# The MLP of a hybrid transformer block rewritten as one ordered sequence of 224 block products

## The chip, the core and the metric

One core of a Trainium2 chip runs the whole block. TensorE (PE in the profile) multiplies into PSUM; VectorE (DVE), ScalarE (ACT) and GpSimd (POOL) work on tiles of 128 partitions; SyncE (SP) issues nearly all DMA transfers, some are issued by ScalarE. The metric is device time in microseconds for one execution, median of three runs.

## The reference

One layer: norm, a mixer (attention and a linear recurrence) with output projection, norm, and an MLP with squared ReLU. Sequence and model width are 1024, the MLP is 4096 wide, all in float32.

```python
def rms_norm(x, g):
    xf = x.astype(jnp.float32)
    y = xf * lax.rsqrt(jnp.mean(xf * xf, axis=-1, keepdims=True) + EPS)
    return (y * g.astype(jnp.float32)).astype(x.dtype)
...
def sq_relu_mlp(h, w_up, w_down):
    return jnp.square(jax.nn.relu(h @ w_up)) @ w_down
...
        h = rms_norm(x, norm1_g[l])
        x = x + hybrid_mixer(h, w_in[l], conv_w[l], conv_b[l], w_rg[l], b_rg[l], w_ig[l], b_ig[l],
                             lru_lambda[l], q_norm_g[l], k_norm_g[l], w_out[l])
        h = rms_norm(x, norm2_g[l])
        x = x + sq_relu_mlp(h, w_up[l], w_down[l])
```

## The kernel before, in words

Every float32 product is made of three matmuls. Each operand is split into a high part (a cast to fp32r by ScalarE) and a low part (operand minus high part, by VectorE or GpSimd); low x high, high x low and high x high are summed in PSUM (`mm3`, lines 62 to 65; `mmc`, lines 602 to 605).

Up to some 450 us the kernel runs the input projection, the recurrence and the attention; its results go to a DRAM buffer `mix_d`. Then comes the output projection (lines 532 to 575): for two column halves `n` and eight token tiles `t`, weights `wr_o` and mixed rows `mr` are loaded through a ring of four tiles of 1024 columns (pool `raws`), split, multiplied into a bank `po`, and added to `x`, which stays in SBUF as `x1`. In the second half, after every second token tile, `x1` is transposed and scaled into `h2` (the MLP's input, model width on partitions), and the row norms go to `rs2`.

The MLP works on blocks. Both `h2 @ w_up` and the product with `w_down` are 2 x 2 block products done with seven block multiplications instead of eight (Strassen-Winograd), for two groups `g` of 2048 MLP columns. So sums and differences of blocks of weights and of `h2` have to be built before they are split, and results are combined in `U` (8 x 4 tiles of 512 columns) or, on the way down, in PSUM and `x1`. Here `hb(k, t, u)` is a piece of `h2`: model half `k`, token half `t`.

Up group (lines 626 to 715), three passes of eight steps `j`: `t2`, `t1`, `t3` with summed weights; `b11`, `b22`, `b21` with plain or reloaded weights (`s2_d` in DRAM); `t4`. Evictions are spread over ScalarE and VectorE; the squared ReLU is `relu2` (line 633). Down group (lines 719 to 804), four passes of eight steps `k`: `da`, `db`, `dd`, `df`. Here the banks `pa` (four) collect several products, `pb` or `pc` (four) one; `acc` (line 732) adds a finished bank to `x1`.

Raw loads, high and low parts are pairs of 512 columns in one tile of 1024 (`raw`, `pair`, `split`); low parts go to VectorE, and every third of some to GpSimd (`lo_eng`, line 597). The rings: four raw tiles, six moving pairs, three stationary pairs.

The order on each engine is set by the framework: it takes the program's instructions, simulates a timeline, and puts each engine's instructions in the order of that timeline. Engines then run in order and wait on semaphores. Tiles that are laid over memory of released pools wait until the former users are done.

## Time and profile before

| what | value |
|---|---|
| median of three runs | 1246.22 us (1245.65 to 1248.36) |
| profiled execution: own time | 1246.13 us |
| profiled execution: span | 1244.3 us |
| PE busy | 1145.4 us (92%), 5410 matmuls |
| DVE busy | 898.2 us (72%) |
| ACT busy | 574.6 us (46%) |
| POOL busy | 657.8 us (53%) |
| granted TensorE clock, mean | 0.966 |
| first MLP matmul, last MLP matmul's eviction | 578.69 us, 1237.83 us |

The span is counted from the first to the last instruction; the execution's own time is a little more. "Busy" counts a matmul from its start to its modelled end, and matmuls overlap, so a busy share near 100% is not a pitch. A row of a timeline has start, duration, engine, line, operation, output and inputs, and in brackets how long the engine sat idle before it and what ended the wait. A row of a window has the stretch, its length, busy time and instruction count for each engine, the granted clock, the DMA share and GB/s.

### The profile page before, as it was taken

How to read it: one execution, taken by the hardware profiler on the slowest of the kernel's cores; microseconds unless marked ns; L12 is line 12 of the kernel's file. 1: busy time of each engine (PE TensorE's matmuls, PEld its weight loads, DVE VectorE, ACT ScalarE, POOL GpSimd, SP SyncE). 2: the span in 40 equal slices, each digit the busy share in tenths (PEclk: the TensorE clock that was granted, in tenths of full speed). 3: DMA queues.
4: the chain of work that ended last, by engine and by line, in shares of the span. 5: the costliest groups of instructions: out<-in, count | busy, mean ns of one | idle time of the engine just before them, and what ended most of it. 6: DMA issues, size and time to landing. Idle time of an engine off the chain costs nothing.

```text
span 1244.3 us, 15625 instructions
## 1 busy us (share of the span) xinstructions
PE 1145.4 (92%) x5410; PEld 940.1 (76%) x5410; DVE 898.2 (72%) x1248; ACT 574.6 (46%) x1023; POOL 657.8 (53%) x552
## 2 busy tenths in 40 slices
PE   8998899899999969973999997999989899989998
PEld 7876687789887658863877876878868688768786
DVE  6889998999988865236466676876954756968744
ACT  7555466566655641243354543243333544523331
POOL 1366654644465743015346679744533475996450
PEclk9999999999999879996998998999999899989999
DMA  8210011401010833002433252455134223425633
GB/s 257 56 39 35 35 47 33 133 10 49 10 33 27 276 111 133 1 1 101 127 94 93 68 169 93 159 177 161 53 127 129 83 79 125 135 94 170 196 134 119
DMA packets 80144, 123.55 MB, mean 99 GB/s; under 512 B 9616, under 2 KB 28096, under 8 KB 80064
## 3 DMA queue, kind: packets, MB, share of 16 engines
q1 hardware_dynamic: 75456, 114.15, 29.3%
q10 hardware_dynamic: 4608, 8.39, 1.7%
q8 instruction: 43, 0.70, 0.2%
q14 instruction: 37, 0.30, 0.1%
HBM read 103.64 MB, written 18.88 MB: 98 GB/s over the span
## 4 chain that ended last, share of the span: by engine, by line
PE 46%; DVE 19%; POOL 11%; DMA 9%; issue 8%; ACT 5%; SPq 1%; POOLq 0%; ACTq 0%; DVEq 0%
PE p L605 16%; PE pa L605 6%; PE po L63 2%; DVE g L415 2%; PE po L65 2%; PE po L64 2%; PE pc L605 2%; POOL U L637 2%; PE pd L63 2%; PE pd L64 2%; PE pd L65 2%; DMA de<-in_w_down_dram 1%; PE pb L605 1%; PE av L435 1%; DMA dc<-in_w_down_dram 1%
## 5 line engine op out<-in xcount | busy, mean ns | idle before, releaser
L416 POOL TENSOR_TENSOR w<-w,g 128x128 f32<-128x128 f32 (+3 forms) x96 | 100.0, 1051 | 102.8 <-DVE g L415 52.5
L415 DVE TENSOR_TENSOR_SCAN g<-g 128x128 f32<-128x128 f32 (+3 forms) x96 | 112.0, 1179 | 6.2 <-ACT g L410 4.6
L63 PE MATMUL pd<-wh_p,hTl 128*128 128x384 f32 x256 | 91.1, 357 | 9.5 <-DVE vv L180 5.0
L64 PE MATMUL pd<-wl_p,hTh 128*128 128x384 f32 x256 | 89.9, 351 | 0.3
L65 PE MATMUL pd<-wh_p,hTh 128*128 128x384 f32 x256 | 87.9, 343 | 0.0
L637 POOL TENSOR_TENSOR U<-U 128x512 f32<-128x512 f32 x48 | 67.9, 1417 | 36.5 <-ACT U L635 34.4
L605 PE MATMUL p<-mh_t,sl_s 128*128 128x512 f32 x128 | 50.4, 401 | 28.2 <-DVE sl_s L60 24.6
L605 PE MATMUL p<-mh_b,sl_a 128*128 128x512 f32 x128 | 52.1, 407 | 9.5 <-DVE U L690 9.5
L660 POOL TENSOR_TENSOR rq<-rs,rq 128x512 f32<-128x512 f32 x16 | 22.3, 1397 | 72.5 <-DMA rq<-in_w_up_dram 72.5
L430 ACT CAST wth<-pw 128x512 fp32r<-128x512 f32 (+1 forms) x80 | 42.6, 548 | 38.5 <-PE pw L426 26.8
L410 ACT ACTIVATE g<-z 128x128 f32<-128x128 f32 (+3 forms) x96 | 48.1, 501 | 25.9 <-PE z L408 11.0
L63 PEld LDWEIGHTS pd<-wh_p,hTl 128*128 128x128 f32 x256 | 49.2, 192 | 13.6 <-DVE vv L180 6.7
L60 DVE TENSOR_TENSOR wtl<-pw,wth 128x512 fp32r<-128x512 f32 (+1 forms) x80 | 49.5, 629 | 12.0 <-ACT wth L430 11.5
L426 PE MATMUL pw<-ident,w 128*128 128x128 f32 x288 | 48.7, 288 | 3.9 <-POOL w L416 1.8
L605 PE MATMUL p<-ml_b,sh_a 128*128 128x512 f32 x128 | 51.6, 403 | 0.0
L605 PE MATMUL p<-mh_b,sh_a 128*128 128x512 f32 x128 | 51.5, 402 | 0.0
L64 PEld LDWEIGHTS pd<-wl_p,hTh 128*128 128x128 f32 x256 | 49.3, 193 | 2.7 <-issue 1.4
L605 PE MATMUL p<-ml_t,sh_s 128*128 128x512 f32 x128 | 50.8, 397 | 0.0
L605 PE MATMUL p<-mh_t,sh_s 128*128 128x512 f32 x128 | 50.8, 397 | 0.0
L605 PEld LDWEIGHTS p<-mh_t,sl_s 128*128 128x128 f32 x128 | 24.8, 194 | 34.0 <-DVE sl_s L60 24.9
L60 DVE TENSOR_TENSOR sl_a<-ra,sh_a 128x1024 fp32r<-128x1024 f32 x16 | 24.8, 1550 | 35.1 <-ACT sh_a L516 35.1
L65 PEld LDWEIGHTS pd<-wh_p,hTh 128*128 128x128 f32 x256 | 49.1, 192 | 1.2 <-issue 1.2
(367 smaller groups left out, 3909.6 us busy)
## 6 DMA issues: line engine op xcount, KB each, us to landing
rs<-in_w_up_dram SPq DMA_DIRECT2D x32, 256.0 KB, 2.7
ra<-in_w_up_dram SPq DMA_DIRECT2D x16, 512.0 KB, 3.7
da<-in_w_down_dram SPq DMA_DIRECT2D x32, 256.0 KB, 3.5
db<-in_w_down_dram SPq DMA_DIRECT2D x32, 256.0 KB, 2.7
dd<-in_w_down_dram SPq DMA_DIRECT2D x32, 256.0 KB, 2.6
wr_p<-in_w_in_dram SPq DMA_DIRECT2D x24, 192.0 KB, 2.7
xt<-in_x_dram SPq DMA_DIRECT2D x8, 512.0 KB, 6.5
wr_o<-in_w_out_dram SPq DMA_DIRECT2D x8, 512.0 KB
```

The costliest lines, as they stand in the source:

```text
L60: eng.tensor_tensor(lo, src, hi.bitcast(F32), op=ALU.subtract)
L63: nc.tensor.matmul(ps, al, bh, start=start, stop=False)
L64: nc.tensor.matmul(ps, ah, bl, start=False, stop=False)
L65: nc.tensor.matmul(ps, ah, bh, start=False, stop=stop)
L410: nc.scalar.activation(g[:, :kn], z, AF.Sigmoid, scale=-1.0)
L415: nc.vector.tensor_tensor_scan(gr, gr, gr, g[:, kn:kn + 1], op0=ALU.mult, op1=ALU.bypass)
L416: nc.gpsimd.tensor_tensor(w[:, :kn], w[:, :kn], g[:, 1:kn + 1], op=ALU.mult)
L426: nc.tensor.transpose(pw[:, i * P:(i + 1) * P], wrow[rr][j // 4][:, j % 4 * P:(j % 4 + 1) * P], ident)
L430: nc.scalar.copy(wth[:, :nw], pw[:, :nw])
L605: nc.tensor.matmul(ps, x_, y_, start=start and n == 0, stop=stop and n == 2, skip_group_check=True)
L637: nc.gpsimd.tensor_tensor(c, c, c, op=ALU.mult)
L660: nc.gpsimd.tensor_tensor(q[:, 1], r[:, 1], q[:, 1], **add)
```

## The change

The MLP becomes one list of 224 block products of 12 matmuls each (`Product`; 112 per group), fed by `Item`s that load 1 to 4 raw tiles. All raw tiles, stationary parts and moving parts are now 512 columns wide and live in rings of 8, 6 and 12. After each product's matmuls the program writes its eviction, attached work, the sum for the product eight ahead, the stationary split six ahead (which also issues the loads for which tiles are free) and, on the way down, the moving split four ahead. From the fifth product on every instruction of PE, DVE, ACT, POOL and SP is kept in that written order (`keep_in_program_order`); the first four are still placed by the framework.

All high parts are ScalarE's, all low parts VectorE's. The passes are regrouped. Up: `b11`/`b21` (16 products, plain weights), `t2`/`b22`/`t3` (24, one item of four loads per `j`), `t1`/`t4` (16). The spill of `s2_d` is gone. Down: `da`/`db` (16), `ea`/`eb` (16), `ga`/`gc` (16), `ha` (8).

Before that, `mlp_head` is called in the output projection ahead of token tile 4 of the second half: it loads and splits the first operands there. For this the memory around the output projection is laid out anew: its raw ring has three tiles (was four), each weight piece has a pair of its own, and the rings lie on the right side of memory, over the last attention tiles. The removed bodies of `up_group` and `down_group` are printed above and are not repeated here.

```diff
-    rwp = pool(ctx, "raws", bufs=4)
-    mvp = pool(ctx, "moving", bufs=6)
-    stp = pool(ctx, "stationary", bufs=3)
+    raws = pool(ctx, "ra", bufs=4, side="right")
+    early = ExitStack()
+    wf = pool(early, "wf", bufs=4, side="right")
+    rwp = pool(early, "raws", bufs=3, side="right")
     tail = ExitStack()
+    wn0 = pool(tail, "wn0")
+    wn1 = pool(tail, "wn1")
+    junk = pool(tail, "junk").tile([P, D], F32, name="junk")
+    wn2 = pool(tail, "wn2", bufs=2)
     mxp = pool(tail, "mix")
     mixes = [(mxp.tile([P, KC, 512], F32R, name=f"mix{g}h"), mxp.tile([P, KC, 512], F32R, name=f"mix{g}l")) for g in range(2)]
+    wpools = {(0, u): wf for u in range(4)} | {(1, 0): wn0, (1, 2): wn1, (1, 3): wn2, (1, 1): wn2}
...
+    def wpair(n, u):
+        t = wpools[n, u].tile([P, 2, 2, 512], F32R, tag="w", name=f"wo{n}{u}")
+        return t[:, 0], t[:, 1]
...
+    MAHEAD, UAHEAD, WLAG, PINNED = 4, 8, 2, 4
+    pinned = False
...
+    rwr, stp, mvp = Ring(4, 4), Ring(3, 3), Ring(8, 4)
+    rwr.pools[0] = raws
+    class Engine:
+        def __init__(self, eng):
+            self.eng = eng
+        def __getattr__(self, op):
+            def call(*args, **kw):
+                ins = getattr(self.eng, op)(*args, **kw)
+                return tc.keep_in_program_order(ins) if pinned else ins
...
+    def split2(pl, name, src):
+        h, l = half(pl, name)
+        act.copy(h, src)
+        dve.tensor_tensor(l, src, h.bitcast(F32), **sub)
+        return h, l
...
+    QA, QB = (ps_z, ps_z, ps_d, ps_d), (ps_w, ps_w, ps_a, ps_t)
...
+    def mmc(ps, st, mv, start, stop):
+        for n, (x_, y_) in enumerate(((1, 0), (0, 1), (0, 0))):
+            pe.matmul(ps, st[x_], mv[y_], start=start and n == 0, stop=stop and n == 2, skip_group_check=True)
...
+        def load(self, q):
+            self.raws = [rwr.tile([P, 512], F32, tag="r", name=f"r_{name}") for name, _ in self.srcs]
+            for t, (_, src) in zip(self.raws, self.srcs):
+                sp.dma_start(t, src)
+            self.at = q
...
+            def mm():
+                b = ps()
+                for kc in range(4):
+                    c = slice(kc * P, kc * P + P)
+                    mmc(b, (pr.st[0][:, c], pr.st[1][:, c]), movs[f"{g}{key}"][kc], start and kc == 0, stop and kc == 3)
...
+        def pa_(j):
+            prod(its[j], 0, "b11", bks[j], lambda: act.copy(U[:, j, 1], bks[j]()), True, False, 1)
+        def pb_(j):
+            prod(its[j], 1, "b21", bks[j], lambda: relu2(j, 0, bks[j]()), False, True, 1)
+        pa_(0)
+        for j in range(1, 8):
+            pa_(j)
+            pb_(j - 1)
+        pb_(7)
...
+            after(q0 + 7 + u, lambda u=u: mov(f"{g}t2", u, U[:, u, 3]))
+            after(q0 + 9 + u, lambda u=u: dve.scalar_tensor_tensor(U[:, 4 + u, 2], U[:, u, 3], -1.0, hb(0, 0, u), op0=ALU.mult, op1=ALU.subtract))
+            after(q0 + 13, lambda u=u: mov(f"{g}b22", u, hb(1, 1, u)))
+            after(q0 + 15, lambda u=u: mov(f"{g}t3", u, U[:, 4 + u, 2]))
+        for j in range(8):
+            def sums(r):
+                tt(gps, r[1], r[1], r[0], **add)
+                tt(gps, r[2], r[2], r[1], **add)
+                tt(dve, r[3], r[3], r[2], **add)
+            it = Item([(f"sa{g}{j}", w(1, 0, j)), (f"sb{g}{j}", w(0, 0, j)), (f"sc{g}{j}", w(1, 1, j)), (f"sd{g}{j}", w(0, 1, j))], sums)
+            ITEMS.append(it)
+            ps, ps1 = banked(f"p2_{g}{j}"), banked(f"p3_{g}{j}")
+            prod(it, 2, "t2", ps, lambda j=j, ps=ps: tt(dve, U[:, j, 2], ps(), U[:, j, 1], **add), True, False, 1)
+            prod(it, 3, "b22", ps1, lambda j=j, ps1=ps1: tt(dve, U[:, j, 2], ps1(), U[:, j, 2], **add), True, True, 1)
+            prod(it, 1, "t3", ps, lambda j=j, ps=ps: tt(dve, U[:, j, 1], ps(), U[:, j, 1], **add), False, True, 2)
...
+            after(q0 + 21, lambda u=u: mov(f"{g}t1", u, hb(0, 1, u)))
+            after(q0 + 22, lambda u=u: mov(f"{g}t4", u, U[:, 4 + u, 3]))
+        for j in range(8):
+            it = Item([(f"ta{g}{j}", w(1, 0, j)), (f"tb{g}{j}", w(1, 1, j))], lambda r: tt(gps, r[0], r[0], r[1], **add))
+            ITEMS.append(it)
+            ps, ps1 = banked(f"p4_{g}{j}"), banked(f"p5_{g}{j}")
+            def ev(j=j, ps=ps):
+                tt(dve, U[:, j, 3], ps(), U[:, j, 1], **sub)
+                tt(dve, U[:, j, 2], U[:, j, 2], ps(), **sub)
+                relu2(j, 3)
+                relu2(j, 2, eng=gps)
+            def ev1(j=j, ps1=ps1):
+                tt(dve, U[:, j, 1], ps1(), U[:, j, 1], **sub)
+                relu2(j, 1)
+            prod(it, 0, "t1", ps, ev, True, True, 1)
+            prod(it, 1, "t4", ps1, ev1, True, True, 1)
...
+            it = Item([(f"da{g}{k}", wd(0, k, 0)), (f"db{g}{k}", wd(0, k, 1))], lambda r: tt(gps, r[1], r[1], r[0], **add))
+            ITEMS.append(it)
+            prod("pa", 0, k, "da", True, False, it, 0, 1, lambda: acc(sets["pa"], 0, 0, rs2))
+            prod("pb", 2, k, "db", True, False, it, 1, 1, lambda: acc(sets["pb"], 1, 1, rs2),
+                 lambda k=k: tt(gps, U[:, k, 2], U[:, k, 2], U[:, k, 3], **sub))
+        for k in range(8):
+            def sums(r):
+                tt(gps, r[0], r[0], r[1], **add)
+                tt(gps, r[0], r[0], r[2], **add)
+            it = Item([(f"ea{g}{k}", wd(0, k, 1)), (f"eb{g}{k}", wd(0, k, 0)), (f"ec{g}{k}", wd(1, k, 1))], sums)
+            ITEMS.append(it)
+            prod("pa", 2, k, "ea", False, False, it, 0, 2, lambda: acc(sets["pa"], 0, 1, nrs2),
+                 lambda k=k: tt(dve, U[:, k, 2], U[:, k, 2], U[:, k, 0], **sub), r2_d[g][k])
+            prod("pb", 0, k, "eb", False, True, it, 2, 1, lambda: acc(sets["pb"], 0, 1, rs2, True),
+                 lambda k=k: tt(gps, U[:, k, 0], U[:, k, 1], U[:, k, 2], **add))
+        for k in range(8):
+            it = Item([(f"ga{g}{k}", wd(1, k, 1)), (f"gb{g}{k}", wd(0, k, 1)), (f"gc{g}{k}", wd(1, k, 0))],
+                      lambda r: tt(gps, r[0], r[0], r[1], **add))
+            ITEMS.append(it)
+            prod("pa", 2, k, "ga", False, False, it, 0, 2, lambda: acc(sets["pa"], 1, 1, nrs2, True),
+                 lambda k=k: dve.scalar_tensor_tensor(U[:, k, 2], U[:, k, 2], -1.0, U[:, k, 3], op0=ALU.mult, op1=ALU.subtract))
+            prod("pc", 1, k, "gc", True, True, it, 2, 1, lambda: acc(sets["pc"], 0, 0, rs2, True))
...
+            it = Item([(f"ha{g}{k}", wd(1, k, 0)), (f"hb{g}{k}", r2_d[g][k])], lambda r: tt(gps, r[0], r[0], r[1], **add))
+            ITEMS.append(it)
+            prod("pa", 3, k, "ha", False, True, it, 0, 2, lambda: acc(sets["pa"], 1, 0, rs2, True))
...
+    def load_items(q):
+        nonlocal free, nload
+        while nload < min(limit, len(ITEMS)) and free >= len(ITEMS[nload].srcs):
+            ITEMS[nload].load(q)
+            free -= len(ITEMS[nload].srcs)
+            nload += 1
+    def stat(n):
+        nonlocal free
+        if n < len(PR):
+            pr = PR[n]
+            pr.item.add()
+            pr.stat()
+            if pr.mov is None:
+                free += pr.free
+        load_items(n - NSTAT)
+    def moving(n, q):
+        nonlocal free
+        if n < len(PR) and PR[n].mov is not None:
+            PR[n].item.add()
+            PR[n].mov()
+            free += PR[n].free
+        load_items(q)
+    def mlp_head():
+        early.close()
+        mvp.pools[0] = pool(ctx, "ma", bufs=8, side="right")
+        stp.pools[0] = pool(ctx, "sa", bufs=3, side="right")
+        load_items(-NSTAT)
+        for u in range(4):
+            mov("0b11", u, hb(0, 0, u))
+        for n in range(3):
+            stat(n)
+        for u in range(4):
+            mov("0b21", u, hb(1, 0, u))
...
+            if n == 1 and grp[0] == 4:
+                mlp_head()
...
-                    wo[u] = split((nc.gpsimd, nc.vector)[(u + n) % 2], pair(stp if n == 0 and u != 1 else mvp, f"o{n}{u}"), wr)
+                    wo[u] = split((nc.gpsimd, nc.vector)[(u + n) % 2], wpair(n, u), wr)
...
+    for pl, nm, n in ((rwr, "rb", 4), (stp, "sb", 3), (mvp, "mb", 4)):
+        pl.pools[1] = pool(ctx, nm, bufs=n)
...
+    limit = len(ITEMS)
+    load_items(-NSTAT)
+    for n in range(3, NSTAT):
+        stat(n)
+    for q, pr in enumerate(PR):
+        pinned = q >= PINNED
+        pr.mm()
+        pr.ev()
+        for fn in pr.after:
+            fn()
+        if q + UAHEAD < len(PR) and PR[q + UAHEAD].usum is not None:
+            PR[q + UAHEAD].usum()
+        stat(q + NSTAT)
+        moving(q + MAHEAD, q)
+        for it in ITEMS[:nload]:
+            if it.at <= q - WLAG:
+                it.add()
```

How this moves instructions, at three places. First, PE between the output projection (`po17` is its last bank, `pth` the transposes of `x1`) and the MLP. Before (`p6_00` is the first MLP bank):

```order
L65 MATMUL po17_6058<-mh_o11_5740,mix1h_5427 128x512
L566 MATMUL pth5_3_6004<-ident_79,x1_5411 128x128 x4
L566 MATMUL pth7_0_6085<-ident_79,x1_5411 128x128 x4
L566 MATMUL pth7_1_6092<-ident_79,x1_5411 128x128 x4
L566 MATMUL pth7_2_6099<-ident_79,x1_5411 128x128 x4
L566 MATMUL pth7_3_6106<-ident_79,x1_5411 128x128 x4
L605 MATMUL p6_00_6189<-mh_t200_6152,sl_s00_6185 128x512
```

After:

```order
L65 MATMUL po17_6109<-wo11_5749,mix1h_5440 128x512
L577 MATMUL p1_00_6230<-m0b110_5949,sb110_5961 128x512 x3
L577 MATMUL p1_00_6230<-m0b111_5952,sb110_5961 128x512 x3
L577 MATMUL p1_00_6230<-m0b112_5955,sb110_5961 128x512 x2
L905 MATMUL pth5_3_6057<-ident_79,x1_5411 128x128 x4
L905 MATMUL pth7_0_6136<-ident_79,x1_5411 128x128 x4
```

The first product (`m0b11`: parts of the first token half, `sb110`: parts of a plain weight block) now stands directly behind the projection, with the last transposes among the products.

Second, SP around the end of the attention, whose last outputs are the stores from `ob313` and `ob303`. Before, the first loads of the projection stand well ahead of them:

```order
L541 DMA wr_o00_5432<-in_w_out_dram 128x2x512
L546 DMA mr00_5438<-mix_d_87 128x2x512
L443 DMA mix_d_87<-ob213_4675 64x256
L467 DMA mix_d_87<-hl30_5329 128x512
L541 DMA wr_o02_5460<-in_w_out_dram 128x2x512
L546 DMA mr02_5466<-mix_d_87 128x2x512
```

After, they come behind both stores and behind four loads of the MLP:

```order
L443 DMA mix_d_87<-ob313_5103 64x256
L577 DMA r_a00_5941<-in_w_up_dram 128x512
L577 DMA r_b00_5942<-in_w_up_dram 128x512
L443 DMA mix_d_87<-ob303_5202 64x256
L577 DMA r_a01_5945<-in_w_up_dram 128x512
L577 DMA r_b01_5946<-in_w_up_dram 128x512
L880 DMA wr_o00_5448<-in_w_out_dram 128x2x512
L885 DMA mr00_5453<-mix_d_87 128x2x512
```

Third, the `t1`/`t4` pass after the change, VectorE (`p4`, `p5`: banks of the two products of a step; `st10`, `st41`: low parts for products six ahead):

```order
L577 TENSOR_TENSOR U_6199<-p4_01_7150,U_6199 128x512
L577 TENSOR_TENSOR U_6199<-U_6199,p4_01_7150 128x512
L577 TENSOR_TENSOR st10_7169<-r_ta04_6999,st10_7169 128x512
L577 TENSOR_TENSOR U_6199<-p5_01_7172,U_6199 128x512
L577 TENSOR_TENSOR st41_7188<-r_tb04_7000,st41_7188 128x512
```

and ScalarE in the same step (the rows of `U` are relu, square, relu, then relu, square):

```order
L577 ACTIVATE U_6199<-U_6199 128x512 x3
L577 CAST st10_7169<-r_ta04_6999 128x512
L577 ACTIVATE U_6199<-U_6199 128x512 x2
L577 CAST st41_7188<-r_tb04_7000 128x512
L577 ACTIVATE U_6199<-U_6199 128x512 x3
```

Each low part follows its cast, and each relu its subtract, in the same place of both rows. Before, VectorE's subtracts of the last up pass (`L714`) stood in ones and twos between splits of 1024 columns, as the framework's timeline had placed them.

316 lines of the change are left out of this document (123 added, 193 removed).

## The prediction

> **What bounds the kernel now.** I read the windows first, cut at the stages, with TensorE beside the others.
>
> ```profile
> core 0: us, PE busy (x) PEld busy (x) DVE busy (x) ACT busy (x) POOL busy (x), PEclk, DMA share, GB/s
> 500.00:552.00 52.00, 51.09 (x252) 42.20 (x251) 12.04 (x46) 18.70 (x41) 0.00 (x0) 1.00 0.00 0
> 552.00:579.00 27.00, 1.62 (x9) 1.15 (x10) 23.09 (x26) 10.19 (x16) 16.55 (x7) 0.61 0.11 39
> 648.00:720.00 72.00, 67.04 (x286) 54.77 (x285) 48.79 (x50) 33.11 (x50) 45.88 (x33) 0.95 0.30 88
> 720.00:776.00 56.00, 47.97 (x200) 38.25 (x199) 39.48 (x31) 23.12 (x28) 51.91 (x29) 0.94 0.39 127
> 776.00:820.00 44.00, 43.01 (x187) 34.63 (x187) 37.98 (x29) 14.72 (x15) 30.96 (x17) 1.00 0.44 150
> ```
>
> Between the output projection and the MLP, TensorE is idle for a whole window of 27 us. Inside the MLP it is nearly full. The chain of waits gives its true pitch and the MLP's ends, and the table of waits names the hole:
>
> ```profile
> 578.69 61.08 PE p L605 x262
> 1188.15 2.72 PE pc L605 x12
> 1237.83 2.79 DVE x L737 x4
> PE p L605 <- DVE sl_s L60: 24.6, 1, 24.6
> ```
>
> Twelve matmuls take 2.72 us, 0.2267 each. The MLP has 224 block products of 12, or 2688 matmuls: 609.3 us at that pitch. It runs from 578.69 to 1237.83, 659.1 us, so 49.8 us are lost inside it. The hole at its head (24.6 us of waiting, then nothing but transposes) comes on top. Those two sums are all that the change can win, since the 2688 matmuls stay.
>
> **Part 1, the hole at the head: 26.7 us less.** The timeline gives the end of the output projection:
>
> ```profile
> 549.17 0.39 PE L65 MATMUL po<-mh_o,mix1h 128*128 128x512 f32 x1
> 549.40 1.03 PE L566 MATMUL pth<-ident,x 128*128 128x128 f32 x8
> 550.93 0.66 PE L566 MATMUL pth<-ident,x 128*128 128x128 f32 x4 [0.49 <-ACT h L569]
> 552.69 1.39 PE L566 MATMUL pth<-ident,x 128*128 128x128 f32 x8 [1.11 <-ACT h L569]
> ```
>
> Now the first product waits for sums of both token halves, a split on three engines, and loads. In the change the first products multiply plain weight blocks by the first token half, whose parts are made while the projection's last token groups run; the order puts them directly behind the last matmul of the projection. Of 578.69 - 549.40 = 29.3 us only the 20 transposes stay, 20 x 0.13 (1.03 / 8) = 2.6. Bounds: -29.3 if these are covered, -20 if ScalarE, which still has the last token scalings there, is late for the first splits. I take -26.7.
>
> **Part 2, the head of the output projection: 5.7 us more.** Before, two weight loads and two mix loads are issued at 411.7 to 414.5, while attention runs; ScalarE casts them at once when attention ends:
>
> ```profile
> 411.69 0.43 SPq L541 DMA_DIRECT2D wr_o<-in_w_out_dram  x1
> 414.49 0.54 SPq L546 DMA_DIRECT2D mr<-mix_d  x1
> 447.01 5.00 SPq L443 DMA_DIRECT2D mix_d<-ob  x2
> 450.98 1.04 ACT L516 CAST sh_o<-wr_o 128x1024 fp32r<-128x1024 f32 x1
> 455.57 0.39 SPq L541 DMA_DIRECT2D wr_o<-in_w_out_dram  x1
> 455.59 2.07 PE L63 MATMUL po<-sh_o,mix0l 128*128 128x512 f32 x4 [4.92 <-DVE mix0l L60]
> 459.22 1.05 ACT L516 CAST sh_o<-wr_o 128x1024 fp32r<-128x1024 f32 x1 [4.36 <-DMA wr_o<-in_w_out_dram]
> 460.58 1.05 ACT L548 CAST mix0h<-mr 128x1024 fp32r<-128x1024 f32 x1 [0.31 <-DMA mr<-mix_d]
> L60 DVE TENSOR_TENSOR mix0l<-mr,mix0h x2: 2534/2960/3387, 453.0 to 455.5; 128x1024 fp32r<-128x1024 f32 x2
> ```
>
> The change puts these tiles over the attention's memory, and their loads stand on SP behind the last attention store (ends 452.0) and two small loads. First weight load at 452.0 + 2 x 0.4 = 452.8; it lands 3.65 later (455.57 to 459.22). The mix load behind it, issued at 453.2, lands after 4.5 (the one behind 455.57 was there at 460.58), at 457.7; cast 1.05, low part on VectorE 2.53 while GpSimd splits the weights: 461.3 against 455.59. The ring has three load tiles instead of four, but 24 matmuls (5.4 us) per weight piece cover the next load. So +5.7; bounds 0 (the loads start during attention after all) and 12 (each of the next pieces late as well).
>
> **Part 3, inside the MLP.** All splits are now 512 wide and written in order: ScalarE casts, VectorE subtracts. The operations, one line each:
>
> ```profile
> L714 DVE TENSOR_TENSOR U<-p,U x16: 673/678/686, 726.0 to 1081.5; 128x512 f32<-128x512 f32 x16
> L769 DVE TENSOR_TENSOR U<-U x16: 684/1518/1779, 741.4 to 1115.6; 128x512 f32<-128x512 f32 x16
> L60 DVE TENSOR_TENSOR sl_x<-rb,sh_x x16: 675/680/1179, 647.3 to 1041.8; 128x512 fp32r<-128x512 f32 x16
> L770 POOL TENSOR_TENSOR U<-U x16: 1256/1482/2286, 749.7 to 1117.4; 128x512 f32<-128x512 f32 x16
> L635 ACT ACTIVATE U<-U x48: 613/632/638, 656.6 to 1082.2; 128x512 f32<-128x512 f32 x48
> L618 ACT CAST sh_v<-rs x16: 614/623/626, 571.3 to 968.4; 128x512 fp32r<-128x512 f32 x16
> rs<-in_w_up_dram SPq DMA_DIRECT2D x32, 256.0 KB, 2.7
> L661 POOL TENSOR_TENSOR rq<-rs,rq 128x512 f32<-128x512 f32 x16 | 27.7, 1734 | 1.2
> ```
>
> (Source view: least, median and greatest ns.) A product is 2.72 us of TensorE. Per engine the MLP's operations fit well: 392 splits and some 220 sums on VectorE at 0.68 are 416 us, 520 ScalarE operations at 0.63 are 328, some 184 GpSimd operations at 1.26 are 232, all under 609. So the stalls can only come from order, pass by pass.
>
> *The t1/t4 pass (16 products, twice).* Per two products VectorE must do subtract, subtract, low part, subtract, low part; ScalarE relu, square, relu, cast, then relu, square, cast. Each low part waits for a cast that stands behind the relus, and each relu for a subtract behind the low part before. So the two take turns: 0.68 + 3 x 0.63 + 0.62 + 0.68, then 0.68 + 2 x 0.63 + 0.62 + 0.68 = 7.11 us, where 24 matmuls take 5.44. The last bank is freed by the second subtract of the eighth pair, 7 x 7.11 + 4.55 = 54.3 us after the pass's first product; three low parts of the next pass stand before it (2.0), and eight low parts for t1 and t4 make VectorE about 3 late at the start: 59.3. TensorE wants that bank (fourth of the second down product) after 15 x 2.72 + 2.72 + 2.04 = 45.6. It waits 13.7. Bounds: 8.7 without the two additions, 20 if the 16 low parts each lose 0.4 to GpSimd. I take 15, twice: 30. What is late behind it is VectorE's splits of the down pass, six and four products ahead, which cover some 4 us.
>
> *The second down pass (16 products, twice).* 40 two-input VectorE operations and 24 GpSimd sums. The row of L769 (two inputs in SBUF) runs from 684 to 1779, that of L714 (one in PSUM) never over 686: the first kind waits for GpSimd and GpSimd for it. In turns they need 40 x 0.68 + 24 x 1.26 = 57.4 us against 43.5. The old pass had the same GpSimd sums and half as many operations of double width, and its window (776 to 820) shows 187 matmuls, 42.4 us of work, in 44: sums done ahead absorbed the rest. The new ring holds eight 512-wide tiles, so less runs ahead. Bounds 0 and 14; I take 5, twice: 10.
>
> *The t2/b22/t3 pass (24 products, twice).* A ring of eight tiles holds two items of four, so a loop closes per item: low part frees a tile, load 2.7, GpSimd sum 1.26 to 1.73 twice, VectorE sum 0.68, eviction 0.68, next low part 0.68: 7.3 to 8.2 us against 8.16. I take 2.5 for its start, where t3's parts delay VectorE: 5 in all. Bounds 0 and 22 per pass, below. For the other passes and changes of pass 3 in all.
>
> Sum: 48 us of stalls in place of 49.8, so -1.8. The written order removes some waits and makes one of its own of the same size.
>
> **All together.** 1244.3 + 5.7 - 26.7 - 1.8 = 1221.5 of span. The profiled execution took 1246.13, 1.83 more than its span, and the median of the runs is 1246.22, the same to 0.1. Forecast: 1223.3, say 1223 us, 1.9% faster.
>
> **The rivals.**
>
> *Saturated.* The lead of six stationary parts and eight banks swallows the turns of the t1/t4 pass; 10 us of stalls remain: 1223 - 38 = 1185. For it: 328 and 416 us of work against 609. Against: the turns are a chain, not a load, and the bank that ends it is one product ahead, not eight.
>
> *The memory port decides.* If two-input VectorE work and GpSimd always exclude each other, the second down pass loses its full 14 us instead of 5: 1223 + 18 = 1241. For it: the spread of L769. Against: the old pass lost 1.6 with nearly the same sum.
> [...]
>
> *Slower: the loop over the ring.* If three loads in flight land as late as those of the old third down pass, and GpSimd's sums and the low parts run contended, the loop is 4.4 + 2 x 1.73 + 1.18 + 0.68 + 1.18 = 10.9 us per item (1.18 is the greatest of sl_x), 2.75 over the 8.16 of TensorE, 22 us a pass instead of 2.5: 1223 + 39 = 1262.
>
> ```profile
> de<-in_w_down_dram SPq DMA_DIRECT2D x16, 256.0 KB, 4.4
> ```
>
> It decides from 23 / 16 = 1.4 us per item over TensorE's 8.16 and the 0.3 of the start, a loop of 9.9. For it: only two items fit, and an in-order VectorE that waits for the sum holds the eviction that TensorE needs 2.72 us later. Against: w_up loads landed in 2.7.
>
> *The overlap does not happen.* The first parts lie in memory of the projection's first weights; if they come free late, or the splits starve, the 24.6 us stay: 1223 + 25 = 1248. Against: the order has ScalarE's casts for them among the token scalings of the third and fourth token groups.
>
> **Chances.** Forecast 0.45, saturated 0.17, port 0.14, loop 0.16, no overlap 0.08. About 0.2% is what a measurement of this kernel can tell from no change, 1243.7 to 1248.7. Forecast and saturated are faster, and of the port's case two thirds; the rest of it and a sliver of the last are the same; loop and most of the last are slower: faster 0.72, same 0.06, slower 0.22. The forecast's own range, stalls of 30 to 65, is 1205 to 1240. For 8 in 10 I go down to 1192, leaving half of the saturated case out, and up to 1256, leaving most of the loop out.
>
> **What would show it.** Right: the first MLP matmul within 4 us of the last of the projection; the projection starting near 461; in the t1/t4 passes TensorE idle some 15 us at the start of the first down pass, put down to VectorE's subtract, and VectorE and ScalarE waiting for each other. Wrong: no wait there (saturated); idle spread over the t2/b22/t3 pass with VectorE waiting for GpSimd and GpSimd for loads (loop); low parts over 1.2 us in the median through the second down pass (port); a hole of 20 us before the MLP (no overlap).

## The result, and the profile after

| | before | after |
|---|---|---|
| median of the runs | 1246.51 us (1245.65 to 1248.36) | 1234.68 us (1230.48 to 1236.72) |
| ratio to before, 95% interval | | 0.9899, [0.9867, 0.9931] |
| profiled execution, span | 1244.3 us | 1228.7 us |
| attention's last work (projection's start less its wait) | 450.7 | 446.9 |
| wait for the projection's first low part | 4.9 | 12.3 |
| output projection, first to last matmul | 93.6 | 95.6 |
| last projection matmul to first MLP product | 29.5 | 0.2 |
| MLP, first to last matmul | 660.7 | 669.4 |

The change made the kernel about 1.0% faster; the forecast was 1223 us, 1.9%. The rows of the table are starts of matmuls in the two profiled executions. The hole at the MLP's head is gone, 29.3 us. It was paid back in three places: a later start of the projection (7.4), a longer projection (2.0) and a longer MLP (8.7). Attention ended 3.7 us earlier, in code that the change does not touch; in the profiled executions of the runs below that point lies anywhere from 446.9 to 453.8, so kernels are compared by stages.

The table of TensorE's waits after (total us, times, longest):

```profile
PE pa L577 <- ACT mda L577: 12.6, 2, 6.4
PE po L63 <- DVE mix0l L60: 12.3, 1, 12.3
PE p L577 <- DVE U L577: 6.6, 2, 4.3
PE pb L577 <- DVE U L577: 6.2, 2, 3.3
PE pa L577 <- DVE mda L577: 3.0, 2, 1.5
```

The 24.6 us that led this table before are gone. In their place stand waits of the first down products (`pa`, `pb`), the longer one of the projection (`po`), and one at the first `t3` product of each group (`p`). The timeline shows the head of the MLP closed up; the transposes stand among the first products:

```profile
554.84 0.39 PE L65 MATMUL po<-wo,mix1h 128*128 128x512 f32 x1
555.07 1.99 PE L577 MATMUL p<-m0b,sb 128*128 128x512 f32 x8
556.89 1.03 PE L905 MATMUL pth<-ident,x 128*128 128x128 f32 x8
```

The windows of group 0, one per pass (the t1/t4 pass is 672 to 723, the first down pass 723 to 775, the second 775 to 822):

```profile
601.00:672.00 71.00, 68.68 (x291) 55.28 (x289) 46.78 (x63) 22.55 (x39) 25.96 (x19) 0.98 0.38 112
672.00:723.00 51.00, 44.83 (x194) 36.04 (x192) 27.19 (x39) 27.81 (x48) 21.81 (x16) 0.97 0.23 67
723.00:736.00 13.00, 8.49 (x23) 6.17 (x24) 8.81 (x10) 5.62 (x11) 6.17 (x6) 0.71 0.14 40
...
775.00:822.00 47.00, 44.67 (x193) 35.76 (x192) 45.03 (x53) 18.77 (x32) 34.49 (x17) 1.00 0.48 148
822.00:866.00 44.00, 44.00 (x192) 35.82 (x192) 35.13 (x46) 18.70 (x32) 18.08 (x10) 1.00 0.51 171
```

Three places lose time: around 723 and, less, in the t2/b22/t3 pass (601 to 672) and the second down pass. But look at the windows without a wait: 822 to 866 is full and holds 192 matmuls in 44.0 us, 0.2292 each, where the forecast had 0.2267. The chain of waits shows the same in a block of twelve, 2.80 us instead of the 2.72 of before:

```profile
736.49 2.80 PE pa L577 x12
```

So I took the step from one MLP matmul to the next out of the trace, start to start, for all 2688. Steps over 260 ns are waits or a slow clock (427 ns in both traces where the granted clock is 0.50); the rest should be 226.7.

| profiled execution | waits and slow clock, us | mean of the other steps, ns | their excess over 226.7, us |
|---|---|---|---|
| before | 50.9 | 227.0 | 0.7 |
| after | 50.1 | 230.6 | 10.2 |

The excess, 9.5 us more than before, is as large as the whole growth of the MLP (8.7). Nothing in the forecast allowed for it.

### The profile page after: what moved, and what is told of

Same layout as the page of the kernel before. It is cut to its first block, busy times and chain, and to the rows that moved or that the text cites. A ratio compares the mean times of both kernels' runs of the same rounds, so it can differ in the third digit from the quotient of the medians.

```text
span 1228.7 us, 16111 instructions
## 1 busy us (share of the span) xinstructions
PE 1152.3 (94%) x5410; PEld 939.5 (76%) x5410; DVE 921.1 (75%) x1458; ACT 603.2 (49%) x1203; POOL 554.0 (45%) x506
## 4 chain that ended last, share of the span: by engine, by line
PE 60%; DVE 19%; issue 8%; ACT 7%; DMA 3%; POOL 2%; SPq 0%; DVEq 0%; ACTq 0%; POOLq 0%
PE p L577 18%; PE pa L577 11%; PE pb L577 4%; PE pc L577 4%; ACT U L577 3%; PE po L63 3%; PE po L64 2%; PE po L65 2%; DVE U L577 2%; PE pd L63 2%; PE pd L64 2%; PE pd L65 2%; DVE g L415 2%; PE av L435 2%; PE z L406 1%
## 5 line engine op out<-in xcount | busy, mean ns | idle before, releaser
L577 PE MATMUL p<-m1t,st 128*128 128x512 f32 x384 | 91.6, 398 | 4.3 <-DVE U L577 4.3
L577 PE MATMUL p<-m0t,st 128*128 128x512 f32 x384 | 91.9, 398 | 2.3 <-DVE U L577 2.3
L577 DVE TENSOR_TENSOR U<-p,U 128x512 f32<-128x512 f32 x80 | 54.9, 686 | 47.0 <-PE p L577 47.0
L577 PEld LDWEIGHTS p<-m1t,st 128*128 128x128 f32 x384 | 73.1, 191 | 21.5 <-issue 4.7
L577 ACT ACTIVATE U<-U 128x512 f32<-128x512 f32 x96 | 58.9, 629 | 60.9 <-DVE U L577 59.5
L577 PEld LDWEIGHTS p<-m0t,st 128*128 128x128 f32 x384 | 73.1, 191 | 19.8 <-issue 2.7
L577 PE MATMUL p<-m1b,sb 128*128 128x512 f32 x288 | 68.1, 393 | 1.8 <-ACT U L577 1.8
L577 PE MATMUL p<-m0b,sb 128*128 128x512 f32 x288 | 68.7, 394 | 0.0
L577 PE MATMUL pa<-mda,sda 128*128 128x512 f32 x192 | 54.0, 434 | 15.6 <-ACT mda L577 12.6
L577 PEld LDWEIGHTS p<-m1b,sb 128*128 128x128 f32 x288 | 54.0, 188 | 14.5 <-ACT U L577 2.3
L410 ACT ACTIVATE g<-z 128x128 f32<-128x128 f32 (+3 forms) x96 | 48.1, 501 | 27.2 <-PE z L408 15.7
```

The costliest lines, as they stand in the source:

```text
L410: nc.scalar.activation(g[:, :kn], z, AF.Sigmoid, scale=-1.0)
L577: ins = getattr(self.eng, op)(*args, **kw)
```

## The experiments

Times are medians; ratios are to the kernel before, run beside it. "After" stands for the changed kernel, 0.9899.

### Without the turns

The forecast's largest term was the t1/t4 pass: VectorE's low part waits for a cast that stands behind relus which wait for VectorE. Here the low parts of that pass are written one product later than their casts.

```diff
     def split2(pl, name, src):
         h, l = half(pl, name)
         act.copy(h, src)
-        dve.tensor_tensor(l, src, h.bitcast(F32), **sub)
+        late.append(lambda: dve.tensor_tensor(l, src, h.bitcast(F32), **sub))
+        if not lag:
+            lows(late)
...
         pr.ev()
+        lows(late)
+        lag = q % 112 in range(40, 56)
```

> The changed kernel, but in the t1/t4 pass (products 40 to 55 of each group) the low part of each split on VectorE is written one product later than its cast on ScalarE, so that VectorE does not wait there for a cast that stands behind relus which wait for VectorE. The same operations, each engine's own work unchanged. Theory 'turns' (the forecast's): in that pass VectorE and ScalarE take turns, 7.1 to 7.3 us per pair of products where TensorE takes 5.44, and the debt of 14.8 us per group shows at the first down products. Without the turns the pair is bound by TensorE; 14.8 us falls to 0 to 4 per group: 1235 - 22 to 30 = 1205 to 1213 us (ratio 0.967 to 0.974). Rival 'load': the engines are simply short of time there, because two-input sums on VectorE and GpSimd's sums shut each other out (1.78 us instead of 0.68); then the pass still loses over 10 us per group and the time stays within 5 us of 1235.

Measured: 1200.83 us, 0.9636 [0.9597, 0.9676]. VectorE's timeline in the pass, first after, then of this run:

```profile
704.29 0.69 DVE L577 TENSOR_TENSOR st<-r_tb,st 128x512 fp32r<-128x512 f32 x1 [1.87 <-ACT st L577]
704.90 0.68 DVE L577 TENSOR_TENSOR U<-p,U 128x512 f32<-128x512 f32 x1
705.50 0.68 DVE L577 TENSOR_TENSOR U<-U,p 128x512 f32<-128x512 f32 x1
707.98 1.12 DVE L577 TENSOR_TENSOR st<-r_ta,st 128x512 fp32r<-128x512 f32 x1 [1.80 <-ACT st L577]
709.02 0.68 DVE L577 TENSOR_TENSOR U<-p,U 128x512 f32<-128x512 f32 x1
711.57 0.69 DVE L577 TENSOR_TENSOR st<-r_tb,st 128x512 fp32r<-128x512 f32 x1 [1.87 <-ACT st L577]
```

```profile
700.37 0.69 DVE L578 TENSOR_TENSOR U<-p,U 128x512 f32<-128x512 f32 x1 [0.87 <-PE p L578]
700.98 0.84 DVE L578 TENSOR_TENSOR st<-r_ta,st 128x512 fp32r<-128x512 f32 x1
703.14 0.69 DVE L578 TENSOR_TENSOR U<-p,U 128x512 f32<-128x512 f32 x1 [1.32 <-PE p L578]
703.75 0.68 DVE L578 TENSOR_TENSOR U<-U,p 128x512 f32<-128x512 f32 x1
704.34 0.69 DVE L578 TENSOR_TENSOR st<-r_tb,st 128x512 fp32r<-128x512 f32 x1
```

After, one pair of products takes 711.57 - 704.29 = 7.28 us, and every low part has waited 1.8 to 1.9 us for ScalarE. Here VectorE waits only for TensorE, 0.9 and 1.3 us at a time, and the pair takes 5.5 us (its second row at 703.14 comes again at 708.67), TensorE's pace. TensorE's windows over the same 45 us, after and here:

```profile
716.00:761.00 45.00, 34.32 (x135) 26.72 (x134) 33.77 (x38) 23.09 (x41) 26.57 (x17) 0.89 0.26 73
```

```profile
716.00:761.00 45.00, 45.00 (x197) 36.58 (x196) 42.24 (x40) 21.30 (x38) 29.72 (x19) 1.00 0.41 115
```

The loss at the first down products, 14.2 and 15.9 us in the two groups after, is 0.0 in both. The turns are shown: 30 us of the 50 lost inside the MLP, where no engine is short of time (after, VectorE and ScalarE are busy 27.2 and 27.8 us of the 51 of that pass), came from the place of 40 low parts in the written order, 20 in each group. The time is below the expected 1205 to 1213: from its first to its last matmul the MLP is 31.1 us shorter, and what the medians show beyond that lies outside the MLP or in the spread of the runs.

### The same debt at another place

The forecast had named VectorE's subtract, which frees the fourth bank of product 57, as the wait that shows the debt. TensorE was first stopped elsewhere, by the first moving split of the down pass:

```profile
723.07 0.79 PE L577 MATMUL pa<-mda,sda 128*128 128x512 f32 x1 [6.24 <-ACT mda L577]
725.38 5.06 PE L577 MATMUL pa<-mda,sda 128*128 128x512 f32 x11 [1.52 <-DVE mda L577]
730.24 2.36 PE L577 MATMUL pb<-mdb,sdb 128*128 128x512 f32 x9
735.52 0.96 PE L577 MATMUL pb<-mdb,sdb 128*128 128x512 f32 x3 [2.92 <-DVE U L577]
```

This run moves the two splits forward and leaves the turns.

```diff
-        moving(q + MAHEAD, q)
+        if q % 112 in (49, 50):
+            moving(q + 7, q)
+        elif q % 112 not in (52, 53):
+            moving(q + MAHEAD, q)
```

> The changed kernel, but in each group the splits of the first two moving tiles of the down pass (products 56 and 57) are written three products earlier, behind products 49 and 50; VectorE and ScalarE still take turns. In the changed kernel the first of these tiles was what TensorE waited for at product 56 (6.4 us, then 1.5 to 2.1 for its low part, then a slow clock), and VectorE's subtract, which the forecast had named, came second, at the fourth bank of product 57 (3.1 and 3.5 us). Theory 'turns' (one debt of the pass, which shows wherever it meets TensorE first): the waits at product 56 go, the wait at product 57 grows to 10 to 13 us, and the loss per group stays 13 to 16 us: 1230 to 1236 us. Rival 'late split' (the place of these two splits is the cause): the waits at 56 go and the one at 57 stays near 3 us: 1217 to 1222 us.

Measured: 1235.51 us, 0.9936 [0.9913, 0.996]. The waits at product 56 are gone, and the banks of product 57 take their place one after another:

```profile
724.00 0.94 PE L577 MATMUL pb<-mdb,sdb 128*128 128x512 f32 x3 [2.88 <-ACT U L577]
727.43 1.65 PE L577 MATMUL pb<-mdb,sdb 128*128 128x512 f32 x3 [2.49 <-DVE U L577]
731.19 1.65 PE L577 MATMUL pb<-mdb,sdb 128*128 128x512 f32 x3 [2.11 <-DVE U L577]
736.37 1.65 PE L577 MATMUL pb<-mdb,sdb 128*128 128x512 f32 x3 [3.53 <-DVE U L577]
```

The loss is 15.7 and 16.3 us per group, the same. An earlier split only moves the place where one debt is paid; the rival falls.

### No written order

```diff
-    MAHEAD, UAHEAD, WLAG, PINNED = 4, 8, 2, 4
+    MAHEAD, UAHEAD, WLAG, PINNED = 4, 8, 2, 1 << 30
```

> The changed kernel, products and buffers as they are, but no engine is kept in the written order: the framework's scheduler orders each engine. Theory 'order' (the written order itself makes the turns of VectorE and ScalarE in the t1/t4 pass): the scheduler puts casts ahead of relus that wait, so the loss at the first down products falls from 15 to under 8 us per group, while it may add waits elsewhere, as before the change (49.8 us in all): 1215 to 1245 us, and the loss at that place is what tells. Rival 'work': the loss at that place stays at 14 to 16 us per group whatever the order.

Measured: 1219.42 us, 0.9801 [0.9778, 0.9823], 1% faster than with the written order. The first down products wait for nothing; the first down pass loses 2.2 and 2.1 us, at its last products. But another wait heads TensorE's table, at the start of the second down pass, where the additions that free the banks are late:

```profile
PE pa L577 <- DVE x L577: 16.1, 2, 8.1
```

The waits and slow steps are 36.0 us here, 50.1 with the written order. So the gain of the change is not due to the order being written: products, buffers and tile sizes alone give 2%, and the written order as it stood took half of that back. With one correction of that order (the run without the turns) it beats the framework's.

### The head called after the projection

```diff
             if n == 1 and grp[0] == 4:
-                mlp_head()
...
+    mlp_head()
     tail.close()
```

> The changed kernel with the MLP's head (its first loads, casts and splits) called only after the loop of the output projection instead of before its last four token groups. The memory and the rest stay. Theory of the forecast: the hole of 24.6 us of waiting before the first MLP product was the wait for these first parts, and the overlap with the projection removes it. Undone, the first product waits for loads (2.7 us), four or eight splits in a row (some 8 x 0.63 on ScalarE, 8 x 0.68 on VectorE) behind the last token scalings: a hole of 10 to 25 us, 1245 to 1260 us (ratio 0.999 to 1.011). Rival: the new order of the first products (plain blocks instead of sums) alone removed the hole, and the framework's own order would have brought these parts forward anyway: hole under 4 us, 1235 to 1238 us.

Measured: 1235.99 us, 0.9913 [0.9879, 0.9947], not to be told from after. The timeline is the same: the projection's last matmul starts at 556.92, the first product at 557.15. This part of the program is not pinned, and the framework puts the casts among the projection's groups wherever the call stands. The forecast's reason, half of it, was wrong: it is not the place of the head that closes the hole. What is left is what the first products need, which the next run tests in part.

### First products on the second token half

The same, with the first eight moving tiles from the other token half.

```diff
-            mov("0b11", u, hb(0, 0, u))
+            mov("0b11", u, hb(0, 1, u))
...
-            mov("0b21", u, hb(1, 0, u))
+            mov("0b21", u, hb(1, 1, u))
```

> The changed kernel with the MLP's head called after the output projection (which alone changed nothing: 1236 us) and with the first eight moving tiles made from the second token half of h2 instead of the first; so this leaves the right operands of the first 16 products of group 0 out and multiplies others. The same work otherwise. Theory 'dependence': the hole before the first MLP product went because that product now needs only the first token half and plain weight blocks; if it needs the second half, it waits for the last transposes, token scalings, casts and low parts: the 20 last transposes and their scalings (some 5 us), four casts and low parts of 0.6 and 0.68 and 3 waits between engines: a hole of 6 to 12 us, 1241 to 1247 us (ratio 0.996 to 1.000). Rival 'sums and loads': the hole was the wait for sums and loads of the old first products, which are gone either way: under 3 us, 1235 to 1238 us.

Measured: 1240.68 us, 0.9971 [0.9949, 0.9992]. The timeline between projection and MLP:

```profile
558.55 0.39 PE L65 MATMUL po<-wo,mix1h 128*128 128x512 f32 x1
558.78 1.03 PE L903 MATMUL pth<-ident,x 128*128 128x128 f32 x8
...
562.08 1.72 PE L903 MATMUL pth<-ident,x 128*128 128x128 f32 x8 [1.11 <-ACT h L906]
564.87 5.53 PE L577 MATMUL p<-m0b,sb 128*128 128x512 f32 x13 [1.07 <-ACT m0b L577]
```

A gap of 6.1 us, transposes in it. So dependence on the last tokens is worth 6 of the 29 us. The rest was the chain of sums and wide splits behind them; the trace of before has it on VectorE and GpSimd from 554 to 578 (timeline of VectorE, two of its rows, the last just before the first product):

```profile
554.33 1.22 DVE L646 TENSOR_TENSOR t3r<-h 128x1024 f32<-128x1024 f32 x1 [0.25 <-ACT h L569]
...
577.43 1.21 DVE L60 TENSOR_TENSOR sl_s<-rq,sh_s 128x1024 fp32r<-128x1024 f32 x1
```

No run put those sums back, so their share is read from this trace alone.

### The projection's first loads

```diff
+    nraw = 0
+
     def raw(name):
+        nonlocal nraw
+        nraw += 1
+        if nraw <= 12:
+            return h2[:, (nraw - 1) % 8, :].rearrange("p (a f) -> p a f", f=512)
         return rwp.tile([P, 2, 512], F32, tag="r", name=name)
```

> The changed kernel, but the 12 loads of the first half of the output projection (weights and mixed values) go into h2, which is not used yet and does not lie over memory that attention still reads. So the first loads can start during attention again, as before the change. Theory: the projection's late start (12.3 us of waiting for the first low part instead of 4.9) comes from loads that wait for attention's last reads and stores; with the prefetch back the wait is 4 to 6 us, and the time falls by 5 to 8 us: 1227 to 1230 us (ratio 0.984 to 0.987). Rival: the loads of the mixed values, which come from the last attention store itself, decide the start, and the weights' place makes no difference: within 2 us of 1235.

Measured: 1225.58 us, 0.9837 [0.9802, 0.9873]. The queue issues the first loads at 414.5 and 414.9 again, during attention, and in TensorE's waits the projection's is back at its old length:

```profile
414.50 0.38 SPq L886 DMA_DIRECT2D h<-in_w_out_dram  x1
414.93 0.46 SPq L891 DMA_DIRECT2D h<-mix_d  x1
```

```profile
PE po L63 <- DVE mix0l L60: 4.9, 1, 4.9
```

12.3 - 4.9 = 7.4 us is the price of laying the load tiles over attention's memory. The forecast had 5.7.

### U first in memory

The longer steps follow the slot of a tile in its ring: they come back every 6 products for the stationary and every 12 for the moving tiles, 233 ns in the mean of the slowest class against 228 in the fastest (table under the 64-byte pad). The first suspicion was where the tiles lie.

```diff
+    U = pool(ctx, "units").tile([P, 8, 4, 512], F32, name="U")
     for pl, nm, n in ((rwr, "rb", 4), (stp, "sb", 3), (mvp, "mb", 4)):
         pl.pools[1] = pool(ctx, nm, bufs=n)
-    U = pool(ctx, "units").tile([P, 8, 4, 512], F32, name="U")
```

> The changed kernel with one line moved: U (64 KB per partition) is allocated ahead of the second halves of the three rings instead of behind them, so that all stationary and moving tiles of the MLP lie together (143 to 215 KB) instead of in two groups (79 to 107 and 171 to 215 KB). Not one instruction differs. In the trace of the changed kernel the step from one MLP matmul to the next is 226 to 227 ns in some products and 231 to 236 ns in others, the same ones again every 12 products, and 233 in the mean where the moving tile lies in the upper group and the stationary one in the lower. Theory 'place': the step depends on where the two operands lie. Then nearly all products are at 226.7 again: the mean step over the MLP falls from 230.4 to about 227, 2688 x 3.4 ns = 9 us less, 1226 against 1235 us (ratio to the kernel before 0.983 against 0.990). Rival 'load': the longer steps come from more traffic of the other engines on the memory, which is the same here: 1235 us, and the steps stay at 230.4 in the mean.

Measured: 1233.8 us, 0.9897 [0.9854, 0.9939]; mean step 230.6 ns, excess 10.2 us, slot for slot as after. Moving the tiles together left the steps of every slot as they were; my first explanation fell. The rival, load, foretold this result and is left standing by this run; the next run, in which the engines do the same work, tells against it. The shift was 64 KB exactly, and one property of the addresses had stayed: the tiles of the left pools begin at 32 modulo 256 bytes, those of the right pools at 224. Before the change all MLP tiles lay on the left, at 32.

### A pad of 192 bytes

```diff
+    pool(ctx, "pad").tile([P, 48], F32, name="pad")
     xp1 = pool(ctx, "x1")
```

> The changed kernel with a pad of 192 bytes per partition allocated ahead of x1 on the left side of SBUF, nothing else. Without it the moving and stationary tiles of the left pools begin at 32 modulo 256 bytes and those of the right pools at 224 modulo 256 (before the change all were at 32); with it all begin at 224. The run with U moved shifted the left group by 64 KB, which left this offset alone, and the slow and fast matmul steps stayed slot for slot. Theory 'offset': the step from one matmul to the next is longer (about 233 ns instead of 226.7) where moving and stationary operands differ in this offset. With all equal the mean step over the MLP falls from 230.5 to about 227: 10.2 us of excess goes to about 1, and some 1.5 us in the output projection as well: 1235 - 11 = 1224 us (ratio 0.981 against 0.990). Rival 'sides' (left against right, or a fixed pattern in the instruction stream): the steps stay and so does the time, 1235 us.

Measured: 1226.13 us, 0.9848 [0.9817, 0.988]. In the last pass of group 0 (96 matmuls without a wait) after, and with the pad, from the first row's start to the second's:

```profile
866.52 22.32 PE L577 MATMUL pa<-mha,sha 128*128 128x512 f32 x96
888.68 0.62 PE L577 MATMUL p<-m1b,sb 128*128 128x512 f32 x2
```

```profile
871.74 21.92 PE L578 MATMUL pa<-mha,sha 128*128 128x512 f32 x96
893.50 0.84 PE L578 MATMUL p<-m1b,sb 128*128 128x512 f32 x3
```

22.16 us against 21.76, which is 96 x 226.7 ns. The same trace with steps over the whole MLP: mean 226.9 ns, excess 0.6 us. The MLP takes 661.0 us instead of 669.4; the output projection, whose mixed values lie left and whose weights lie partly right, falls from 95.6 to 94.3. Of the 10 to 11 us expected, the medians show 8.6 and the ratios 6.4 (0.9899 and 0.9848, whose intervals overlap a little), so the time alone would not settle it; the steps do. The cause is the start address, not the side: nothing moved by more than 192 bytes.

### A pad of 64 bytes

> As the run with the pad, but 64 bytes instead of 192: the left tiles begin at 96 modulo 256 bytes, the right ones at 224. The difference is 128 where the changed kernel has 192 and the padded one 0. If only offsets modulo 128 count, the difference is none: mean step 227 ns and 1226 us, as with 192 bytes. If it counts modulo 256 or more, the steps stay at 229 to 236 ns in the mixed products, mean 230 to 231, and 1235 us.

Measured: 1232.12 us, 0.991 [0.9895, 0.9926]; mean step 230.8 ns, excess 10.8 us. The classes of products by the start of moving and stationary tile modulo 256, over the steps within a product:

| moving, stationary | products | after: mean step, ns | moving, stationary | 64-byte pad: mean step, ns |
|---|---|---|---|---|
| 224, 32 | 76 | 233.3 | 224, 96 | 233.0 |
| 32, 224 | 42 | 230.5 | 96, 224 | 233.0 |
| 32, 32 | 28 | 228.8 | 96, 96 | 229.2 |
| 224, 224 | 68 | 228.4 | 224, 224 | 228.0 |

(Ten products whose four moving tiles are of both classes are left out, as are steps over 260 ns. With the 192-byte pad all products are 224, 224, at 226.9; before all were 32, 32, at 227.0.) Offsets that differ by 128 cost as much (233.0 ns) as offsets that differ by 192 (230.5 and 233.3), so offsets do not count modulo 128 alone; whether they count modulo 256 or more was not settled.

That products with equal offsets are not quite at 227 has to do with their neighbours. In the trace of after, 33 of them follow another such product and have 226.9 ns in the mean; the 50 that follow a product with unequal offsets have 229.3 (64-byte pad: 31 at 226.7 and 48 at 229.0). The longer steps run on into the next product: behind a product with unequal offsets the first seven steps have means of 228 to 233 ns in the trace of after, the last four 227 to 228.

### Without GpSimd in the second down pass

```diff
             def sums(r):
-                tt(gps, r[0], r[0], r[1], **add)
-                tt(gps, r[0], r[0], r[2], **add)
+                pass
...
-            prod("pb", 0, k, "eb", ..., lambda k=k: tt(gps, U[:, k, 0], U[:, k, 1], U[:, k, 2], **add))
+            prod("pb", 0, k, "eb", ...)
```

> The changed kernel, but the second down pass of each group (ea/eb) leaves out GpSimd's work: the sums of weight blocks ea + eb + ec and the sums of units for eb (48 operations in all), so those 16 products per group multiply other operands. VectorE's work there stays: 40 two-input operations and the additions from the banks. In the changed kernel VectorE is busy 54.0 of 56 us in that pass (the low parts there take 0.84 to 1.43 us in the mean instead of 0.68), and TensorE loses 2.9 and 2.5 us. Theory 'port' (the forecast's, 5 us per group, measured about 2.7): the losses come from VectorE and GpSimd shutting each other out; without GpSimd VectorE's operations go back to 0.68 us, its busy time in the pass falls to 35 to 40 us and TensorE loses under 1 us per group: 1231 us. Rival 'banks': the losses there are the additions that free the banks at the pass's start (product 73 waits for VectorE's x), and stay at 2.5 us per group with VectorE at 0.68: 1235 us. The time alone can hardly tell 4 us; the waits at products 73 and 82 do.

Measured: 1227.21 us, 0.9853 [0.9822, 0.9884]. TensorE loses nothing in that pass, in either group. VectorE's low parts there (least, median, greatest ns), after and here:

```profile
L577 DVE TENSOR_TENSOR mea<-r_ea,mea x7: 677/1124/1780, 778.2 to 814.4; 128x512 fp32r<-128x512 f32 x7
L577 DVE TENSOR_TENSOR seb<-U,seb x6: 675/1670/1781, 781.4 to 810.9; 128x512 fp32r<-128x512 f32 x6
L577 DVE SCALAR_TENSOR_TENSOR x<-pb,rs,x x4: 734/734/739, 778.8 to 780.8; 128x512 f32<-128x512 f32 x4
```

```profile
L577 DVE TENSOR_TENSOR mea<-r_ea,mea x7: 682/685/1782, 780.5 to 812.0; 128x512 fp32r<-128x512 f32 x7
L577 DVE TENSOR_TENSOR seb<-U,seb x6: 681/692/694, 783.7 to 808.6; 128x512 fp32r<-128x512 f32 x6
L577 DVE SCALAR_TENSOR_TENSOR x<-pb,rs,x x4: 742/742/745, 781.1 to 783.1; 128x512 f32<-128x512 f32 x4
```

And the pass as a window here:

```profile
780.00:824.00 44.00, 44.00 (x193) 35.93 (x192) 32.33 (x48) 18.28 (x32) 4.75 (x4) 1.00 0.57 180
```

VectorE's busy time falls from 45.0 of 47 us to 32.3 of 44. These two low parts grew most of four; over all 26 in that window of the trace after, the median is 0.68 us and ten take over 1.2, so the sign that the forecast had named for the port rival, a median over 1.2, did not come.

Leaving out the sums also takes away what the low parts wait for, but in that window of after VectorE is idle for only 2 us: what it lacks is time, and the longer operations take it. So the port theory holds in this: the losses of that pass come from GpSimd's work beside VectorE's. Their price after is 2.9 and 2.5 us in the two groups, half of the forecast's 5 and far from the rival's 14; in the other runs that leave this pass and the written order as they are, both groups together lose 5.5 to 8.3.

The additions from the banks (`x<-pb`, one input in PSUM) take 0.73 us beside GpSimd's sums and 0.74 without. GpSimd is held up too: after, its sum at 781.81 takes 6.25 us, where the one before it took 1.29, and during it nine of VectorE's low parts and sums run back to back at 0.68.

### All together

Pad, turns and prefetch, and one more edit: the last two moving tiles of `t3` are split one product later, behind the eviction that TensorE waits for there.

```diff
-            after(q0 + 15, lambda u=u: mov(f"{g}t3", u, U[:, 4 + u, 2]))
+            if u < 2:
+                after(q0 + 15, lambda u=u: mov(f"{g}t3", u, U[:, 4 + u, 2]))
...
+        for u in range(2, 4):
+            after(q0, lambda u=u: mov(f"{g}t3", u, U[:, 4 + u, 2]))
```

> The changed kernel with four edits: the 192-byte pad, the low parts of the t1/t4 pass one product later than their casts, the first loads of the output projection into h2, and the last two of the four moving tiles of t3 made one product later (behind the eviction that TensorE waits for at the first t3 product, 2.3 us and a slow clock behind it, twice). If the parts add: 1235 - 33 (turns, measured) - 8 (loads, measured) - 11 (pad, if its theory holds) - 3 to 8 (t3) = 1175 to 1180 us, ratio 0.942 to 0.946. If the pad does nothing, 1186 to 1190 us; if the parts only hide one another's waits, over 1195 us.

Measured: 1180.97 us, 0.9492 [0.9468, 0.9517], 64 us faster than the kernel before that ran beside it and 54 faster than after; 1 us over the expected range. Taken singly, the turns, the loads and the pad gave 34, 9 and 9 us by the medians, 1183 us together, so these parts add up. The edit of `t3` was never run alone. Its windows of the t2/b22/t3 pass and of the first two down passes:

```profile
594.00:661.00 67.00, 65.75 (x291) 54.13 (x290) 45.50 (x63) 22.88 (x39) 25.52 (x19) 1.00 0.38 118
...
705.00:749.00 44.00, 43.98 (x195) 36.15 (x194) 42.28 (x39) 20.88 (x38) 30.35 (x19) 1.00 0.38 115
749.00:796.00 47.00, 44.62 (x194) 36.03 (x194) 45.02 (x53) 18.82 (x33) 34.76 (x17) 1.00 0.46 152
```

In the t2/b22/t3 pass the loss is 1.5 and 0.2 us, against 4.1 and 6.2 after. How much of that is the edit of `t3` is not shown: in the other runs of the written order that leave this pass alone both groups together lose anything from 3.3 to 11.1 us there. The waits differ from execution to execution, and so does the slow clock behind them (last section). The MLP takes 624.9 us; 15.4 are still waits and slow steps, 6.7 of them in the two second down passes, where VectorE is busy 45 of 47 us.

## Where the prediction was right, and which of its steps failed

The direction came as forecast, and 1234.68 us lies within the forecast's own range of 1205 to 1240. The gain is half of what was forecast, 11.8 us instead of 23. The three parts came about mostly by the mechanisms that were named for them; nearly all of the other half went into a pace of the matmuls that the forecast had put down as fixed.

**Part 1, the hole: right, -29.3 and transposes among the products.** The forecast's first MLP matmul fell at 554.9 (461.3 and the projection's 93.6), the measured one at 555.07. That these agree so closely is luck: the projection began 2.0 us earlier than forecast and took 2.0 longer. Of the reasons given, the call's place beside the projection carries nothing, and 6 us of the hole hung on the last tokens. By elimination the plain blocks carry the rest; no run shows that share.

**Part 2, the projection's start: right mechanism, too small.** 7.4 instead of 5.7. That the projection began at 459.3 and not near 461 is due to attention, which ended 3.7 us earlier in that execution.

**Part 3, the stalls: 48 us forecast, 47.9 measured (50.1 less 2.2 around the transposes).** By passes, both groups together:

| term | forecast | measured | run that shows the cause |
|---|---|---|---|
| t1/t4 pass, turns | 30 | 30.1 (14.2 and 15.9) | without the turns: 0 |
| second down pass, port | 10 | 5.4 | without GpSimd: 0 |
| t2/b22/t3 pass | 5 | 10.3 | none alone; 1.7 with all four edits |
| other | 3 | 2.1 | |

That the sum fits to 0.1 us is luck: the port was put 4.6 us too high and the t2/b22/t3 pass 5.3 too low. Only the turns were sized well, by counting: 7.11 us per pair against 7.28 in the trace. The place was read less well. The forecast had the bank of product 57 as the first thing late and the splits of the down pass behind it; in fact a moving split came first, and the bank second. It makes no difference to the sum, as the run with earlier splits shows. The port term was nearly twice too large; that the low parts written ahead absorb more than I allowed is my reading, which no run tests. The t2/b22/t3 term was half of what came: the trace has TensorE waiting at the first `t3` product, behind t3's parts as forecast, but the forecast left out what a wait does to the steps behind it (427 ns for some eight of them, below).

**The step that failed is the floor.** "A product is 2.72 us of TensorE" was taken from the trace of before as a property of the 2688 matmuls, "since the 2688 matmuls stay". They do not stay in time: with rings in two pools of different start offsets a step is 230.6 ns in the mean, 9.5 us more in the MLP and some 1.3 in the projection. In its place the runs show a step that depends on the layout: with all operands at one offset (the 192-byte pad) it is 226.9 ns again. Add the 9.5, the 1.3 and the 1.7 of part 2 to the forecast of 1223, and it is 1235.5, against a median of 1234.68. That sum has to be read with care: the profiled execution took 1230.48 and its attention part was 3.7 us shorter than before's.

**The rivals.** Saturated (1185) fell: the lead of six parts and eight banks did not swallow the turns. What the forecast called the port is there, low parts of 1.78 us beside GpSimd's sums where 0.68 is the least, but small, 5.4 us; that a memory port is behind it is shown by no run. Of the slower loop nothing is to be seen: the t2/b22/t3 pass has no wait beyond its start. The lack of overlap did not occur.

## What to carry to other kernels

Where two engines kept in a written order hand work to each other both ways, write a consumer one step later than its producer; a chain of such handovers cost 30 us here with both engines idle for nearly half of the time, and it is found by counting one period by hand. Before a matmul's pace is taken over from an older layout, compare where its operands begin: a pad of 192 bytes was worth some 10 us here by the steps, and 6 to 9 by the measured times. When tiles move to other memory, ask whose last use their first load now waits for (7.4 us here).
